# Folding the pooling heads' map into the output projection's weights on the chip, in a two-part decoder layer on one core

## The chip, the cores and the metric

One core of a Trainium2 chip runs the whole program. The metric is the device time of one execution in microseconds (us), as the median of several executions. The profiled execution is a single one; its span is the time from its first to its last instruction. The engines are named as in the profile: PE (TensorE, matrix products), DVE (VectorE, elementwise), ACT (ScalarE, activations and copies), POOL (GpSimd), SP (SyncE, which issues most transfers).

## The reference

One layer of width 1024 over 2048 positions, in float32. Cut to what the change touches:

```python
p = h @ w_in                                   # q, k, v, gate, i/f logits, and u: 512 pooling channels
hm = head_rmsnorm(mlstm_chunkwise(...), g_head) * sigmoid(o)
# multiscale_pool: 4 groups of 128 channels, windows 2, 4, 8, 16
mean = (c[:, 1:] - lag) / minimum(pos, w)      # trailing mean of the group
d = stack(mean - u_group)
y = einsum('btgc,gcd->btgd', d, w_pool)        # per-group 128 x 128 map
hp = y * pool_scale                            # per channel
x = x + concatenate([hm, hp], -1) @ w_out      # rows 512 to 1023 of w_out meet hp
```

After it come a gated feed-forward part (width 2816, convolution over positions) and a final norm. Both are untouched.

## The kernel before

Positions are worked on in four blocks (`b` = 0 to 3) of 512. For each block `in_phase` (line 531) runs four input projections, `out_proj` (926) the output projection in two halves; the feed-forward part follows at about 685 us of the profile. The order is: input phase of block 0, input phase of block 1, output projection of block 0, input phase of block 2, and so on; the last two output projections follow each other.

Every float32 product is made of three matmuls. A number is split into a rounded high part (`split_h`, line 92, on ACT) and the rest (`split_l`, 98, on DVE), and `products` (108) adds high x high, high x low and low x high in PSUM. Its three lines 112, 113 and 114 are therefore those of nearly all matmuls.

`project` (239) is the main stream: 16 steps of six matmuls (two products). Weights come in units of 128 x 2 x 512 values (512 KB). In every half of eight steps the first steps split the two units of the next half and start the loads of the two after those (`w_load`, 223, on SP, two buffers).

All other work is in generators, the side streams (`Sides`, 57). After each step `tick` advances each of them to its next `yield`, in the order in which they were added. So the order on each engine is fixed when the program is written out: a side stream's instruction stands between the projection's steps on each engine's queue. Buffers that side streams share are counted in rings (`take`, `give`, line 288): `tmp` has six buffers, `mm` two PSUM banks, `num` two, `prs` two. `take_now` spins ticks without projection steps until its slots are free.

What stands around the change:

- `setup` (451) loads small constants, waits some ticks, takes a `tmp` buffer, loads `w_pool` and splits it into `wp`.
- `norm_scale` (313) loads x and squares it, through `tmp` buffers; `qk_out` (532) evacuates the first projection, with two `tmp` buffers each; `conv` (511) gives them back after a POOL product.
- `chain` (593) computes the gates: small matmuls, DVE and ACT steps, each some ticks behind the one before, then a round trip of two rows through DRAM (`rows`), then four chunks.
- `pool_sums` (829) makes the trailing sums on POOL, subtracts the token (847) and splits the result `d` into a `prs` buffer. `pooling` (857) multiplies `wp` with it, three matmuls for each block and group, and splits the product, scaled by `pool_scale`, into the tile from which the output projection reads (`mix_tile`, 211).
- `heads_out` (879) does the like for the other half, through transposes.
- The tiles `mixT0` to `mixT7` hold that projection's input. Before they are first written, their memory holds the first weights and the first slices of x (`first_tiles`, 205).

Of the kernel before, what the change touches and what calls it, by code (L numbers as in the profile page):

```python
# [6 lines left out]
F32 = mybir.dt.float32  # L7
# [6 lines left out]
P = 128  # L14
SEQ = 2048
D = 1024
KT = D // P
# [66 lines left out]
def trunk(tc, x, xT, w_in, w_gate, w_pool, w_out, w_up, w_down, vecs, cst, out):  # L84
# [19 lines left out]
    def split(h, l, src, scale=None):  # L104
        split_h(h, src, scale)
        split_l(h, l, src, scale)

    def products(o, terms, first=True, last=True, on=False):

        n = len(terms)  # L110
        for i, ((lh, ll), (rh, rl)) in enumerate(terms):
            pe.matmul(o, lhsT=lh, rhs=rh, start=first and i == 0, stop=False, skip_group_check=on)  # L112
            pe.matmul(o, lhsT=lh, rhs=rl, start=False, stop=False, skip_group_check=on)  # L113
            pe.matmul(o, lhsT=ll, rhs=rh, start=False, stop=last and i == n - 1, skip_group_check=on)  # L114
# [7 lines left out]
    def parts(t, *idx):  # L122
        return t[(slice(None), 0) + idx], t[(slice(None), 1) + idx]
# [4 lines left out]
    with ExitStack() as ctx:  # L128
# [12 lines left out]
        def nbank(shape):  # L141
            return psum.tile(shape, F32, tag="num", name="num", bufs=2)
# [4 lines left out]
        def wait(n):  # L147
            for _ in range(n):
                yield
# [62 lines left out]
            return (hT if b == NB - 1 else mixT)[k]  # L212


        units = []
        for b in range(NB):
            units += [w_in[g, kp] for g in range(4) for kp in range(KT // 2)]
            if b:
                units += [w_out[h, kp] for h in range(2) for kp in range(KT // 2)]
        units += [w_out[h, kp] for h in range(2) for kp in range(KT // 2)]  # L220
        raws, whl = {}, {}

        def w_load(n):
# [41 lines left out]
        def until(*flag):  # L265
            while flag not in flags:
                yield
# [20 lines left out]
        def take(ring, n=1):  # L288
            while (slots := reserve(ring, n)) is None:
                yield  # L290
            return slots
# [159 lines left out]
        def setup():  # L451
            slot = reserve("tmp", 1)
            cr = tmp()
            n = C_N - C_TRI
            wgr = cr[:, n:n + KT * 8].rearrange("p (k c) -> p k c", k=KT)
            sp.dma_start(cr[:, 0:n], cst[:, C_TRI:C_N])
            sp.dma_start(wgr, w_gate)
            pool.memset(f(wg), 0.0)
            pool.memset(qk_halo, 0.0)
            for g in range(4):  # L460
                pool.memset(u[g][:, BT:], 0.0)
            pool.memset(C, 0.0)
            pool.memset(f(qd), 0.0)
            for c in chl:
                pool.memset(f(c), 0.0)
            pool.memset(m_now[:, TT:TT + 1], 0.0)
            for t in range(TT):
                pool.memset(f(va[t][:, :, :, DV:]), 0.0)
            yield from wait(8)
            split(wg[:, :, 0:8], wg[:, :, 8:16], wgr)  # L470
            for t in range(TT):
                dve.tensor_copy(va[t][:, 0, :, DV:DV + 1], ones.to_broadcast([P, H, 1]))
            dve.tensor_copy(tri, cr[:, 0:P])
            dve.tensor_copy(tab, cr[:, C_TAB - C_TRI:C_N - C_TRI].rearrange("p (g c) -> p g c", g=4))
            give(slot)
            yield from wait(16)
            slot = yield from take("tmp")
            wpr = tmp()[:, 0:512]
            sp.dma_start(wpr, w_pool)
            yield from wait(6)  # L480
            split(wp[:, 0], wp[:, 1], wpr)
            give(slot)
            yield

        def in_op(b, channels):
            def op(w, kp, j, i):
# [342 lines left out]
        def pool_sums(b):  # L829

            yield from until("u", b)
            yield from until("hs", b)
            for g, win in enumerate(WINDOWS):
                s, m, lo = u[g], 1, HALO - win + 1
                while m < win:
                    lo += m
                    slot = yield from take("tmp")
                    n = tmp()
                    pool.tensor_tensor(out=n[:, lo:], in0=s[:, lo:], in1=s[:, lo - m:HALO + BT - m], op=ALU.add)
                    if m > 1:  # L840
                        give(s_slot)
                    s, s_slot, m = n, slot, 2 * m
                    yield
                d_slot = yield from take("prs")
                if b == 0:
                    dve.tensor_tensor(out=s[:, HALO:2 * HALO], in0=s[:, HALO:2 * HALO], in1=tab[:, g], op=ALU.mult)
                dve.scalar_tensor_tensor(out=s[:, HALO:], in0=s[:, HALO:], scalar=1.0 / win, in1=u[g][:, HALO:], op0=ALU.mult, op1=ALU.subtract)
                d = ph1.tile([P, 2, BT], F32R, tag="prs", name="prs", bufs=2)
                split_h(d[:, 0], s[:, HALO:])
                yield  # L850
                split_l(d[:, 0], d[:, 1], s[:, HALO:])
                give(s_slot)
                state["d", b, g] = d, d_slot
                yield from wait(3)
                flags.add(("d", b, g))

        def pooling(b):
            if b < NB - 1:
                yield from until("op", b - 1)
            for g in range(4):  # L860
                yield from until("d", b, g)
                if b < NB - 1:
                    yield
                slot = yield from take("num")
                d, d_slot = state.pop(("d", b, g))
                o = nbank([P, BT])
                gs = slice(g * P, (g + 1) * P)
                products(o, [((wp[:, 0, gs], wp[:, 1, gs]), parts(d))])
                give(d_slot)
                yield  # L870
                m = mix_tile(b, 4 + g)
                split_h(m[:, 0], o, vec[:, V_PSC + g:V_PSC + g + 1])
                yield from wait(2)
                split_l(m[:, 0], m[:, 1], o, vec[:, V_PSC + g:V_PSC + g + 1])
                give(slot, 1)
                flags.add(("mix", b, 4 + g))
            flags.add(("pool", b))

# [102 lines left out]
        steps = setup()  # L981
        next(steps)
        sides.add(steps)
        scales = {0: sides.add(norm_scale(0))}
        for b in range(NB):
            in_phase(b)
            if b == 0:
                mixT += [per.tile([P, 2, BT], F32R, tag=f"mixT{k}", name=f"mixT{k}") for k in range(KT)]
            sides.add(pool_sums(b))
            sides.add(pooling(b))  # L990
            if b == 0:
                sides.add(heads_out(b))
            elif b < NB - 1:
                out_proj(b - 1)
                sides.add(heads_out(b))
            else:
                sides.add(heads_out(b))
                out_proj(b - 1)
# [666 lines left out]
```

## Time and profile before

| what | value |
|---|---|
| median of 3 runs | 2033.52 us (2030.06 to 2034.94) |
| profiled execution, time | 2033.21 us |
| profiled execution, span | 2031.5 us |
| DVE busy | 1455.8 us (72%) |
| ACT busy | 1023.6 us (50%) |
| POOL busy | 176.2 us (9%) |

A row of a timeline gives the start, the length, the engine, the line, the operation, the tile written and the tiles read, how often it was done in a row, and in square brackets how long the engine was idle ahead of it and who released it. Lengths of matmuls overlap; the distance between two starts is what one costs. The page gives the clock that TensorE was granted in tenths, over slices of 50.8 us:

```profile
PEclk9999999999999999999999999999999999999999
```

### The profile page before, as it was taken

Reading aid. Unit: us, or ns where it says so; the run is one execution under the profiler, and the core shown is the slowest. Engines: PE = TensorE matmul, PEld = TensorE weight load, DVE = VectorE, ACT = ScalarE, POOL = GpSimd, SP = SyncE. Lnnn points to the kernel's source line nnn. Section 1 sums busy time; section 2 is a strip of 40 time slices with the busy share of each in tenths; the row PEclk is TensorE's granted clock in tenths of the full one; section 3 lists DMA queues with packets and bytes.
Section 4 is the critical chain, followed back from the end, with each engine's and each line's share of the span. In section 5 each row is a group of like instructions: output and inputs, shape, how many; then the busy total and the mean of one; then the engine's idle time right before and its main releaser. Section 6 shows DMA issues by size and latency. Waiting matters only on the chain.

```text
span 2031.5 us, 24605 instructions
## 1 busy us (share of the span) xinstructions
PE 1976.3 (97%) x8948; PEld 1622.1 (80%) x8948; DVE 1455.8 (72%) x2371; ACT 1023.6 (50%) x1808; POOL 176.2 (9%) x224
## 2 busy tenths in 40 slices
PE   8989999998999899999999999999999999999997
PEld 6777887776787688888888888888888888888886
DVE  5587788687686978778778566588878778865443
ACT  5655655654654545545546454344544544544331
POOL 1003012111020000000000000000111111000000
PEclk9999999999999999999999999999999999999999
DMA  4433454442435522222224854432322222375341
GB/s 181 155 112 114 138 164 166 154 158 94 169 127 185 199 84 83 94 86 70 94 86 143 283 198 146 165 104 99 109 94 70 86 94 69 134 274 175 119 139 55
DMA packets 121850, 267.56 MB, mean 132 GB/s; under 512 B 10112, under 2 KB 28032, under 8 KB 121728
## 3 DMA queue, kind: packets, MB, share of 16 engines
q1 hardware_dynamic: 114528, 252.87, 37.8%
q10 hardware_dynamic: 7200, 13.11, 1.7%
q8 instruction: 70, 1.15, 0.2%
q14 instruction: 52, 0.43, 0.1%
HBM read 221.32 MB, written 44.63 MB: 131 GB/s over the span
## 4 chain that ended last, share of the span: by engine, by line
PE 80%; DVE 9%; ACT 4%; DMA 3%; issue 2%; SPq 1%; POOL 0%; DVEq 0%; ACTq 0%; POOLq 0%
PE big L112 21%; PE big L113 21%; PE big L114 21%; PE num L114 5%; PE num L113 5%; PE num L112 5%; DVE whl L100 1%; DVE tmp L519 1%; ACT hjunk L819 1%; PE mm L503 1%; DVE hT L102 1%; ACT whl L94 1%; DMA tmp<-in_x 1%; DVE so L825 0%; DVE C L785 0%
## 5 line engine op out<-in xcount | busy, mean ns | idle before, releaser
L112 PE MATMUL big<-s,w 128*128 128x512 f32 (+1 forms) x1562 | 606.1, 388 | 7.1 <-ACT r L1382 7.0
L114 PE MATMUL big<-s,w 128*128 128x512 f32 (+1 forms) x1562 | 603.9, 387 | 0.0
L113 PE MATMUL big<-s,w 128*128 128x512 f32 (+1 forms) x1562 | 603.8, 387 | 0.0
L94 ACT CAST w<-raw 128x512 fp32r<-128x512 f32 (+1 forms) x442 | 272.6, 619 | 505.0 <-PE big L114 355.5
L100 DVE TENSOR_TENSOR w<-raw,w 128x512 fp32r<-128x512 f32 (+1 forms) x442 | 302.1, 685 | 202.5 <-ACT w L94 197.4
L112 PEld LDWEIGHTS big<-s,w 128*128 128x128 f32 x1562 | 293.8, 188 | 71.3 <-ACT r L1382 9.0
L114 PEld LDWEIGHTS big<-s,w 128*128 128x128 f32 x1562 | 293.8, 188 | 60.0
L113 PEld LDWEIGHTS big<-s,w 128*128 128x128 f32 x1562 | 293.7, 188 | 58.3 <-issue 0.7
L1354 DVE SCALAR_TENSOR_TENSOR q<-q,vec 128x1024 f32<-128x1024 f32 x176 | 225.4, 1282 | 22.7 <-ACT q L1351 21.3
L112 PE MATMUL num<-s,w 128*128 128x512 f32 x396 | 154.5, 390 | 0.0
L114 PE MATMUL num<-s,w 128*128 128x512 f32 x396 | 154.2, 389 | 0.0
L113 PE MATMUL num<-s,w 128*128 128x512 f32 x396 | 154.0, 389 | 0.0
L112 PE MATMUL big<-hT,whl 128*128 128x512 f32 x320 | 128.7, 402 | 9.0 <-ACT whl L94 5.6
L100 DVE TENSOR_TENSOR whl<-wraw,whl 128x1024 fp32r<-128x1024 f32 x92 | 114.9, 1249 | 27.4 <-ACT whl L94 26.2
L100 DVE TENSOR_TENSOR s<-x,s 128x512 fp32r<-128x512 f32 x120 | 81.5, 688 | 67.7 <-ACT s L94 67.1
L94 ACT CAST s<-x 128x512 fp32r<-128x512 f32 x120 | 73.1, 619 | 109.7 <-PE big L114 41.9
L113 PE MATMUL big<-hT,whl 128*128 128x512 f32 x320 | 126.8, 396 | 0.9 <-DVE hT L102 0.9
L114 PE MATMUL big<-hT,whl 128*128 128x512 f32 x320 | 126.3, 395 | 0.0
L1375 POOL COPY q<-halo 128x2 f32<-128x2 f32 x88 | 65.3, 759 | 592.0 <-DVE q L1354 298.5
L1351 ACT ACTIVATE q<-q,vec 128x1024 f32<-128x1024 f32 x88 | 109.5, 1244 | 0.0
L112 PE MATMUL big<-whl,hT 128*128 128x512 f32 x256 | 105.6, 412 | 0.0
L113 PE MATMUL big<-whl,hT 128*128 128x512 f32 x256 | 102.7, 401 | 2.0 <-DVE whl L100 2.0
(266 smaller groups left out, 2925.3 us busy)
## 6 DMA issues: line engine op xcount, KB each, us to landing
raw<-in_w_up SPq DMA_DIRECT2D x44, 1024.0 KB, 5.6
raw<-in_w_down SPq DMA_DIRECT2D x35, 1024.0 KB, 5.1
wraw<-in_w_in SPq DMA_DIRECT2D x60, 512.0 KB, 3.4
act<-q SPq DMA_DIRECT2D x44, 512.0 KB, 6.4
x<-act SPq DMA_DIRECT2D x88, 256.0 KB, 3.8
wraw<-in_w_out SPq DMA_DIRECT2D x32, 512.0 KB, 3.5
xr<-in_xT SPq DMA_DIRECT2D x32, 256.0 KB, 4.2
x2d<-xr ACTq DMA_DIRECT2D x32, 256.0 KB, 2.9
```

What stands on the lines that cost most here:

```text
L94: act.copy(out=h, in_=src)
L100: dve.tensor_tensor(out=l, in0=src, in1=f(h), op=ALU.subtract)
L102: dve.scalar_tensor_tensor(out=l, in0=src, scalar=scale, in1=f(h), op0=ALU.mult, op1=ALU.subtract)
L112: pe.matmul(o, lhsT=lh, rhs=rh, start=first and i == 0, stop=False, skip_group_check=on)
L113: pe.matmul(o, lhsT=lh, rhs=rl, start=False, stop=False, skip_group_check=on)
L114: pe.matmul(o, lhsT=ll, rhs=rh, start=False, stop=last and i == n - 1, skip_group_check=on)
L503: pe.matmul(gp, lhsT=wg[:, k], rhs=hT[k][:, i], start=k == 0 and i == 0, stop=k == KT - 1 and i == 1)
L519: dve.scalar_tensor_tensor(out=y, in0=pre[:, n:n + BT], scalar=tap[n], in1=y, op0=ALU.mult, op1=ALU.add)
L819: act.activation(junk, nums[h // 2][:, h % 2, 0:DV], AF.Square, scale=rd[:, h:h + 1], accum_out=ssq[:, h:h + 1])
L1351: act.activation(y[gv], pre[gv][:, 2:2 + HT], AF.Identity, scale=tap[2], bias=vec[:, V_FB + ch:V_FB + ch + 1])
L1354: dve.scalar_tensor_tensor(out=y[gv], in0=pre[gv][:, n:n + HT], scalar=tap[n], in1=y[gv], op0=ALU.mult, op1=ALU.add)
L1375: pool.tensor_copy(t[:, 0:2], halo[:, gv * NJ + j])
```

## The change

Since pooling values go through two linear maps with a scale between them, `w_pool`, `pool_scale` and rows 512 to 1023 of `w_out` can be multiplied once. The new stream `fuse` does this on the chip: four units (two column halves times two pairs of groups), each loaded into a tile of `mixT`'s memory, split, multiplied with the transposed and scaled `wp` (two products for each unit), copied from PSUM by ACT and stored in DRAM (`wpo_d`). The output projection then loads these instead of the last two units of each half of `w_out`. `setup` takes its `w_pool` earlier (4 ticks in place of 16), transposes it by TensorE and splits it with the scale. `pooling` is gone; `pool_sums` splits `d` directly into the projection's input tile, without a `prs` buffer, and waits for the output projection of the block before ahead of the first split. Block 0 ends with `need("fused")`.

```diff
+        wpo_d = [[dram.tile([P, 2, 512], F32, name=f"wpo{h}_{i}") for i in range(2)] for h in range(2)]
+        out_units = [w_out[h, kp] if kp < 2 else wpo_d[h][kp - 2] for h in range(2) for kp in range(KT // 2)]
...
-            yield from wait(16)
+            yield from wait(4)
             slot = yield from take("tmp")
             wpr = tmp()[:, 0:512]
             sp.dma_start(wpr, w_pool)
             yield from wait(6)
-            split(wp[:, 0], wp[:, 1], wpr)
+
+            mm_slot = yield from take("mm")
+            wt = bank([P, BT])
+            for g in range(4):
+                pe.transpose(out=wt[:, g * P:(g + 1) * P], in_=wpr[:, g * P:(g + 1) * P], identity=ident)
             give(slot)
             yield
+            for g in range(4):
+                gs, scale = slice(g * P, (g + 1) * P), vec[:, V_PSC + g:V_PSC + g + 1]
+                split_h(wp[:, 0, gs], wt[:, gs], scale)
+            yield
+            for g in range(4):
+                gs, scale = slice(g * P, (g + 1) * P), vec[:, V_PSC + g:V_PSC + g + 1]
+                split_l(wp[:, 0, gs], wp[:, 1, gs], wt[:, gs], scale)
+            give(mm_slot)
+            flags.add(("wp",))
+            yield
+
+        def fuse():
+
+            def load(n):
+                raw = per.tile([P, 2, 512], F32, tag=f"mixT{4 * (n % 2)}", name="wor")
+                sp.dma_start(raw, w_out[n // 2, 2 + n % 2])
+                return raw
+            yield from wait(14)
+            raws2 = [load(0), load(1)]
+            yield from until("wp")
+            for n in range(4):
+                raw = raws2.pop(0)
+                res = per.tile([P, 2, 512], F32, tag=f"mixT{3 + 4 * (n % 2)}", name="wo")
+                for j in range(2):
+                    w = per.tile([P, 2, 512], F32R, tag=f"mixT{1 + 4 * (n % 2) + j}", name="wos")
+                    gs = slice((2 * (n % 2) + j) * P, (2 * (n % 2) + j + 1) * P)
+                    split_h(w[:, 0], raw[:, j])
+                    yield
+                    split_l(w[:, 0], w[:, 1], raw[:, j])
+                    yield
+                    slot = yield from take("mm")
+                    o = bank([P, 512])
+                    products(o, [(parts(wp, gs), parts(w))])
+                    yield
+                    act.copy(out=res[:, j], in_=o)
+                    give(slot)
+                del raw, w
+                act.dma_start(wpo_d[n // 2][n % 2], res)
+                del res
+                if n < 2:
+                    raws2.append(load(n + 2))
+            flags.add(("fused",))
...
                 dve.scalar_tensor_tensor(out=s[:, HALO:], in0=s[:, HALO:], scalar=1.0 / win, in1=u[g][:, HALO:], op0=ALU.mult, op1=ALU.subtract)
-                d = ph1.tile([P, 2, BT], F32R, tag="prs", name="prs", bufs=2)
+                if b < NB - 1:
+                    yield from until("op", b - 1)
+                d = mix_tile(b, 4 + g)
                 split_h(d[:, 0], s[:, HALO:])
                 yield
                 split_l(d[:, 0], d[:, 1], s[:, HALO:])
                 give(s_slot)
...
-        def pooling(b):
-            if b < NB - 1:
-                yield from until("op", b - 1)
-            for g in range(4):
-                yield from until("d", b, g)
-                if b < NB - 1:
-                    yield
-                slot = yield from take("num")
-                d, d_slot = state.pop(("d", b, g))
-                o = nbank([P, BT])
-                gs = slice(g * P, (g + 1) * P)
-                products(o, [((wp[:, 0, gs], wp[:, 1, gs]), parts(d))])
-                give(d_slot)
-                yield
-                m = mix_tile(b, 4 + g)
-                split_h(m[:, 0], o, vec[:, V_PSC + g:V_PSC + g + 1])
-                yield from wait(2)
-                split_l(m[:, 0], m[:, 1], o, vec[:, V_PSC + g:V_PSC + g + 1])
-                give(slot, 1)
                 flags.add(("mix", b, 4 + g))
             flags.add(("pool", b))
...
+        sides.add(fuse())
...
+                need("fused")
```

## Rows read from the trace of the kernel before

**Rows 1.** The page's totals: busy time, share of the span, instructions.

```profile
PE 1976.3 (97%) x8948; PEld 1622.1 (80%) x8948; DVE 1455.8 (72%) x2371; ACT 1023.6 (50%) x1808; POOL 176.2 (9%) x224
```

**Rows 2.** Timeline of PE around the first pooling product of block 0.

```profile
189.93 0.39 PE L112 MATMUL num<-prs,wp 128*128 128x512 f32 x1
...
190.62 0.60 PE L887 MATMUL mm<-ident,so 128*128 128x128 f32 x4
190.97 0.47 PE L112 MATMUL big<-whl,hT 128*128 128x512 f32 x1
```

**Rows 3.** The tile `wp`, matmuls: lengths in ns, first and last start.

```profile
L112 PE MATMUL num<-prs,wp x16: 392/393/495, 189.9 to 651.8; 128*128 128x512 f32 x16
```

**Rows 4.** Timeline of PE: pooling matmuls with idle time ahead of them.

```profile
374.54 0.49 PE L112 MATMUL num<-prs,wp 128*128 128x512 f32 x1 [1.44 <-ACT prs L94]
376.17 0.50 PE L113 MATMUL num<-prs,wp 128*128 128x512 f32 x1 [1.13 <-DVE prs L100]
...
640.43 0.49 PE L112 MATMUL num<-prs,wp 128*128 128x512 f32 x1 [1.00 <-ACT prs L94]
```

**Rows 5.** Busy time by stretch: PE, PEld, DVE, ACT, POOL, then granted clock, DMA share, GB/s.

```profile
372.00:377.10 5.10, 2.53 (x10) 1.56 (x9) 5.07 (x10) 5.10 (x11) 2.11 (x1) 1.00 0.25 75
377.20:380.50 3.30, 3.30 (x9) 2.58 (x8) 3.13 (x12) 1.21 (x6) 0.00 (x0) 0.50 0.74 230
...
506.90:513.60 6.70, 5.82 (x14) 4.57 (x15) 5.50 (x9) 3.08 (x4) 1.64 (x1) 0.50 0.36 106
```

**Rows 6.** Timeline of PE in blocks 0 and 1.

```profile
38.03 0.39 PE L112 MATMUL big<-whl,hT 128*128 128x512 f32 x1
...
47.03 0.49 PE L626 MATMUL mm<-lfs,tri 128*128 128x16 f32 x2 [2.04 <-ACT lfs L94]
...
54.13 0.27 PE L636 MATMUL mm<-ident,w 128*16 128x128 f32 x1 [1.07 <-DVE w L630]
...
62.39 0.20 PE L658 MATMUL mm<-ones,mrow 1*16 1x1 f32 x2 [0.48 <-DVE mrow L652]
...
76.73 0.38 PE L742 MATMUL mm<-ident,qk 128*128 128x128 f32 x2
...
80.72 0.50 PE L113 MATMUL big<-whl,hT 128*128 128x512 f32 x1 [1.99 <-DVE whl L100]
...
146.92 3.85 PE L503 MATMUL mm<-hT,wg 128*16 128x512 f32 x16
```

**Rows 7.** Timelines of ACT and DVE at the end of the first projection.

```profile
42.33 0.63 ACT L523 ACTIVATE tmp<-tmp 128x512 f32<-128x512 f32 x1
...
44.36 0.17 DVE L541 COPY tmp<-qk_halo 128x3 f32<-128x3 f32 x1 [1.86 <-POOL qk L528]
```

**Rows 8.** The page's groups: DVE's subtraction of a 128 x 512 split.

```profile
L100 DVE TENSOR_TENSOR w<-raw,w 128x512 fp32r<-128x512 f32 (+1 forms) x442 | 302.1, 685 | 202.5 <-ACT w L94 197.4
```

**Rows 9.** Timeline of DVE in the second projection of block 0.

```profile
54.44 0.41 DVE L641 TENSOR_TENSOR_SCAN ml<-mm,ones 16x128 f32<-16x128 f32 x1 [0.45 <-PE mm L636]
...
58.27 0.74 DVE L102 SCALAR_TENSOR_TENSOR va<-big,nr,va 128x512 fp32r<-128x512 f32 x1
...
60.62 1.20 DVE L650 COPY mrow<-mrow 1x4 f32<-1x4 f32 x1
61.74 0.60 DVE L652 TENSOR_TENSOR_SCAN mrow<-mm,mrow,br 1x4 f32<-1x4 f32 x4
```

**Rows 10.** Timelines of SP, ACT and DVE in the third projection of block 0.

```profile
73.31 0.59 SPq L319 DMA_DIRECT2D tmp<-in_x  x1
...
77.15 0.63 ACT L323 ACTIVATE tmp<-tmp 128x512 f32<-128x512 f32 x1 [5.63 <-DMA tmp<-in_x]
...
80.59 0.42 DVE L100 TENSOR_TENSOR qss<-qs,qss 128x256 fp32r<-128x256 f32 x1
```

**Rows 11.** Busy time of 40 to 66 us, columns as in rows 5; the page's transfers.

```profile
40.00:66.00 26.00, 22.41 (x100) 17.20 (x99) 19.16 (x35) 14.57 (x25) 6.08 (x4) 1.00 0.36 117
...
wraw<-in_w_in SPq DMA_DIRECT2D x60, 512.0 KB, 3.4
```

More of the change, by code (lines that the diff above doesn't have):

```diff
@@ L218, in trunk @@
             if b:
-                units += [w_out[h, kp] for h in range(2) for kp in range(KT // 2)]
-        units += [w_out[h, kp] for h in range(2) for kp in range(KT // 2)]
+                units += out_units
+        units += out_units
         raws, whl = {}, {}
@@ L843, in pool_sums @@
                     yield
-                d_slot = yield from take("prs")
                 if b == 0:
@@ L852, in pool_sums @@
                 give(s_slot)
-                state["d", b, g] = d, d_slot
-                yield from wait(3)
-                flags.add(("d", b, g))
-        def pooling(b):
-            if b < NB - 1:
-                yield from until("op", b - 1)
-            for g in range(4):
-                yield from until("d", b, g)
-                if b < NB - 1:
-                    yield
-                slot = yield from take("num")
-                d, d_slot = state.pop(("d", b, g))
-                o = nbank([P, BT])
-                gs = slice(g * P, (g + 1) * P)
-                products(o, [((wp[:, 0, gs], wp[:, 1, gs]), parts(d))])
-                give(d_slot)
-                yield
-                m = mix_tile(b, 4 + g)
-                split_h(m[:, 0], o, vec[:, V_PSC + g:V_PSC + g + 1])
-                yield from wait(2)
-                split_l(m[:, 0], m[:, 1], o, vec[:, V_PSC + g:V_PSC + g + 1])
-                give(slot, 1)
                 flags.add(("mix", b, 4 + g))
@@ L987, in trunk @@
             if b == 0:
+                need("fused")
                 mixT += [per.tile([P, 2, BT], F32R, tag=f"mixT{k}", name=f"mixT{k}") for k in range(KT)]
             sides.add(pool_sums(b))
-            sides.add(pooling(b))
             if b == 0:
```

## The prediction

> **What bounds the kernel now.** I read the page's totals first, then TensorE's timeline with its idle time, then the rows of the pooling matmuls, then the DVE, ACT and SP timelines of the first 90 us. TensorE is busy for 97% of the span [rows 1], so a matmul less is worth its own pitch as long as nothing else is late at that place. The duration of a matmul in the rows is not its pitch, since matmuls overlap: three pooling matmuls start at 189.93 and the next group starts at 190.62, so a product of three costs 0.69 us [rows 2]. The rest of the span is 55 us of idle time, and it lies in a few places, of which two kinds matter here: the pooling matmuls themselves [rows 4], and the first block, where the small matmuls of the gate chain wait for DVE and ACT [rows 6]. The reader should also see the granted clock: after idle stretches of TensorE it falls to 0.50, which is 1.2 GHz, for 3.3 us and for 6.7 us [rows 5]. A stall can so cost twice.
>
> **What the change removes.** The pooling map ran 16 times, three matmuls each [rows 3]: 16 x 0.69 = 11.0 us of TensorE. With them go the waits of these matmuls for their operand, 1.44, 1.13 and 1.00 us [rows 4], together 3.6 us, and the stretch at half clock right behind the first two [rows 5], 3.3 us in which half the work was done, so 1.6 us. These 5.2 us are uncertain. In 372 to 377.1 DVE and ACT are busy nearly without a break [rows 5], so TensorE may meet the same backlog one matmul later; the ends are 0 and 5.2, and I take 5.2, because the split that the pooling matmul waited for leaves TensorE's path altogether. ACT and DVE each lose 16 splits of 128 x 512. I count those as nothing, since neither engine is the bound over these blocks; in the DVE pile-up around 505 to 514 us [rows 5] the pooling splits go, but the last group's sums come earlier, into the same pile; I count 0, with 5 us either way in the range. The new wait in `pool_sums` for the previous output projection holds one `tmp` slot for a few steps; behind it wait only later pool groups, and their result is needed an input projection later, so 0. At the end of the first stage (block 3) the pooled halves are ready earlier; that gives the 1.00 us already counted.
>
> **What the change adds on TensorE.** Four units of two products each: 8 x 0.69 = 5.5 us; four transposes 0.35 us, as the four of 190.62 to 190.97 [rows 2]. Together 5.9 us. The work alone thus gives 11.0 - 5.9 = 5.1 us back.
>
> **Where the added products stand.** This is the step on which the prediction hangs. The side streams are emitted one step per tick, and a tick follows six projection matmuls, twice 0.69, so 1.38 us. `setup` waits 8 + 4 ticks, takes a `tmp` slot (free), loads `w_pool`, waits 6 and so reaches the transposes at tick 18. The third `qk_out` needs that same slot and spins three ticks until then; before, the fourth one spun three ticks for a conv slot. Both versions therefore leave the first projection at tick 20, and the gate chain keeps its places. The flag `wp` comes at tick 20, and `fuse` splits at ticks 20 and 21 and multiplies at 22, then every third tick: 25, 28, 31, 34, 37, 40, 43. A product stands one tick, 1.38 us, behind the DVE subtraction that it needs, and DVE works in order.
>
> First product, tick 22. TensorE gets there two steps into the second projection: 38.03 + 0.35 + 2 x 1.38 = 41.1 us [rows 6]. DVE is then held by the fourth `qk_out`, which needs a buffer that the first conv slice frees on POOL: it resumes at 44.36, behind ACT's sigmoid and its table load [rows 7]. That dependency stays, perhaps 0.7 us earlier. Behind it come the `qk_out` product, four small subtractions for `wp` and the subtraction of the unit (0.69 each) [rows 8]: some 2.6 us, so 46.3. TensorE waits 46.3 - 41.1 = about 5 us. Ends: 3.5 and 6.
>
> At ticks 25 and 28 the operands are there in time, since TensorE has now fallen back. The chain's own waits of 2.04, 1.07 and 0.48 us [rows 6] vanish for the same reason.
>
> Fourth product, tick 31. The chain's scan waits for a matmul of tick 29, then DVE has in order the scan, three conv operations, a weight subtraction and the `va` subtraction, 54.44 to 58.9 [rows 9], and now the unit's 0.69 behind them: 5.2 us from the matmul. TensorE has two steps, 2.8 us, until it needs it: a stall of about 2.5.
>
> Fifth product, tick 34. DVE has a `va` subtraction behind the projection's evacuation, the two operations of 1.20 and 0.60 us of the running maximum [rows 9], a weight subtraction of 1.2 and the unit's own: a stall of about 2.
>
> Eighth product, tick 43. Before, ACT sat idle for 5.63 us until 77.15 for a load of x [rows 10], which SP issued at 73.31 [rows 10] because it was held behind the gate rows' round trip through DRAM. DVE got through with what was queued behind that at about 81.0 [rows 10], while TensorE passed the place of tick 43 one step ahead of the transposes of 76.73 [rows 6], at 75.3. The loads of x run one tick pair earlier without `setup`'s late slot, but the one that ACT needs at tick 40 still follows the rows. With ACT's copy and split and DVE's subtraction behind it I get 81.7 against 75.3; TensorE will come later by about 10 us and the rows by about 9, so a stall of about 5. Ends 2 and 6.5. The 1.99 us at 80.72 [rows 6] go with it.
>
> Sum of the stalls: 5 + 2.5 + 2 + 5 = 14.5, less the 2.04 + 1.07 + 0.48 + 1.99 = 5.6 that they replace: 8.9 us. Ends: 0, if DVE and ACT are ahead of TensorE by these 14.5 us in a way that I don't see, and 13.
>
> The clock: 2.57 us of idle time in 372 to 377.1 was followed by 3.3 us at half clock, and the stall ahead of 507 by 6.7 us [rows 5], while the 2.04 us at 47.03 had no such stretch behind them. Two stalls of 5 us should each be followed by one, at 1.7 to 3.4 us. I take 4 us for both, ends 0 and 8.
>
> **The four loads and stores of the fused units** move 4 MB over some 60 us, on SP's and ACT's queues. In 40 to 66 us the DMA engines are busy for 0.36 [rows 11], so I count 0; SP meets no new long wait, because the tiles that it loads into are free by then. The Trainium skill ("Trainium Kernel Development and Optimization", Key Constraints) says that transfers issued from SP's and ACT's queues all run on the same 16 DMA engines and interleave, which speaks against a count of nothing: each weight unit behind a fused load would land later. By that rule one weight unit late by a landing of another, 3.4 us in the profile's list of issues [rows 11], would cost that much and make the result 2039. The share of 0.36 shows room, so the sum goes by 0.
>
> **Sum against the profiled execution**, which took 2033.2 us with a span of 2031.5; the median of the runs is 0.3 us above: -11.0 - 5.2 + 5.9 + 8.9 + 4 = +2.6. I predict 2036 us.
>
> **Rivals.** (A) The cover holds: DVE and ACT deliver the units in time and only the count of matmuls moves. For it: DVE and ACT are idle between many of their rows, and the first block has buffers to run ahead. Against it: the chain's waits at 47, 54 and 62 us [rows 6], with four or more ticks of distance where the products have one. Time: 2033.2 - 11.0 + 5.9 - 5.2 = 2023, or 2028 if the waits of the pooling matmuls come back elsewhere. (B) Slower: the ladder of stalls in the first block at its upper ends, each stall of 5 us followed by the longer stretch at half clock. 2033.2 - 11.0 + 5.9 + 13 + 8 = 2049 with nothing won at the pooling matmuls, 2044 with it; in the middle 2043. It decides once the first block loses over 22 us, against 19 in my sum. For it: in-order queues make each delay wait for TensorE's next step, and the first block has no slack that gives it back. (C) The stalls come as forecast, but the DVE pile-up at 505 us, with its stretch of 6.7 us at half clock, thins out because the last pool group's POOL additions no longer run under it: 5 us better, 2031.
>
> **How the numbers follow.** Forecast 0.40, with 2030 to 2039 as its own range; A 0.20; B 0.28; C 0.12. This kernel's measurement tells about 0.3%, 6.1 us, from no change: faster below 2027.4, slower above 2039.6. A lies mostly below (0.16 of its 0.20), B above; the forecast leaks 0.02 to each side. Faster 0.18, same 0.52, slower 0.30. The range of 2023 to 2045 leaves out half of A and a quarter of B.
>
> **What would show it.** In the changed kernel: 48 matmuls with `wp` as weights gone from blocks 0 to 3 and 24 there between 41 and 95 us; idle rows of TensorE ahead of products with result tile `mm`, released by DVE or ACT, of about 5, 2.5, 2 and 5 us; a granted clock of 0.50 behind the first and the last; the 16 gate matmuls of block 1, at 146.92 before [rows 6], later by 15 to 22 us, and the rest of the first stage then shorter by some 16. If the fused products show no idle time ahead of them, the step with the ticks is wrong and A holds.

## The result, and the profile after

The changed kernel takes 2042.63 us (median of 6 runs, 2037.49 to 2044.54), the kernel before beside it 2031.8 us (6 runs). The ratio is 1.0054, with a 95% interval of [1.0042, 1.0065]: slower by some 11 us, by more than the 0.3% that the prediction set as its bound. The predicted 2036 us is 6.6 us too low; the time lies inside the stated 2023 to 2045 and outside the forecast's own 2030 to 2039. The profiled execution took 2043.11 us, with a span of 2041.4 against 2031.5, so 9.9 us longer.

The page's totals after, to be read against [rows 1]:

```profile
PE 1976.8 (97%) x8928; PEld 1621.1 (79%) x8928; DVE 1453.4 (71%) x2366; ACT 1023.1 (50%) x1811; POOL 175.1 (9%) x224
```

There are twenty matmuls fewer, as the diff says (48 less 28), and yet TensorE is busy for as long as before: the work saved was eaten by work done slowly. To see where, I cut the first stage at the first matmul of each projection on TensorE's timeline. Lengths are in us. In the kernel before, the four pooling products of a block, three matmuls each, ran while the next block was worked on. The first column of numbers is the change that the prediction's terms give. Below, "block 0" stands for the first of these stretches, "block 1" for the second.

| stretch | predicted | before | after | change |
|---|---|---|---|---|
| block 0, second and third projection | +18.8 | 53.6 | 67.5 | +13.8 |
| block 0, fourth projection, and block 1 | -2.8 | 151.1 | 146.5 | -4.7 |
| output projection of block 0 | 0 | 59.4 | 59.2 | -0.3 |
| block 2 | -7.0 | 106.7 | 118.8 | +12.1 |
| output projection of block 1 | 0 | 60.7 | 58.5 | -2.2 |
| block 3 | -2.8 | 114.8 | 108.6 | -6.2 |
| last two output projections | -3.8 | 102.1 | 102.4 | +0.3 |

Before these stretches 0.9 us were won, and in the feed-forward part 2.2.

**Block 0.** Timeline of PE, the fused products with idle time ahead of them:

```profile
44.41 0.80 PE L112 MATMUL mm<-wos,wp 128*128 128x512 f32 x1 [4.38 <-ACT wos L94]
...
64.89 0.50 PE L113 MATMUL mm<-wos,wp 128*128 128x512 f32 x1 [1.92 <-DVE wos L100]
...
71.19 0.50 PE L113 MATMUL mm<-wos,wp 128*128 128x512 f32 x1 [0.92 <-DVE wos L100]
...
77.16 0.50 PE L113 MATMUL mm<-wos,wp 128*128 128x512 f32 x1 [0.57 <-DVE wos L100]
...
88.62 0.50 PE L112 MATMUL mm<-wos,wp 128*128 128x512 f32 x1 [1.44 <-ACT wos L94]
89.52 0.50 PE L113 MATMUL mm<-wos,wp 128*128 128x512 f32 x1 [0.40 <-DVE wos L100]
```

The waits of [rows 6] at 47, 54, 62 and 81 us are gone, and in their place stands the forecast ladder. Busy time by stretch (columns as in [rows 5]) shows the clock behind its first and its last stall, and, in the last three lines, in block 2:

```profile
43.60:50.40 6.80, 5.99 (x13) 4.43 (x14) 5.36 (x10) 4.40 (x8) 1.88 (x1) 0.50 0.33 102
88.60:95.40 6.80, 6.38 (x28) 5.02 (x29) 2.76 (x5) 3.90 (x9) 0.32 (x1) 1.00 0.48 162
...
333.70:337.10 3.40, 3.40 (x9) 2.67 (x9) 3.30 (x6) 1.70 (x3) 2.12 (x2) 0.50 0.49 141
354.20:357.60 3.40, 3.15 (x9) 2.52 (x10) 2.54 (x6) 1.89 (x3) 0.68 (x1) 0.50 0.72 228
384.90:391.70 6.80, 5.90 (x16) 4.63 (x16) 6.11 (x17) 4.25 (x10) 0.00 (x0) 0.50 0.56 189
```

Behind the stall of 4.38 us TensorE ran at 0.50, that is 1.2 GHz, for 6.8 us; behind the last stall, 1.44 and 0.40 us at 89, it stayed at 2.4 GHz.

**Block 2** is the surprise. Timeline of PE there; before, the block's waits were 0.45, 0.35 and the two of [rows 4], 3.4 us together, with one stretch of 3.3 us at half clock:

```profile
333.40 0.36 PE L674 MATMUL mm<-lfs,tri 128*128 128x16 f32 x2 [1.65 <-DVE mixT L102]
...
354.45 0.21 PE L686 MATMUL mm<-bs,ident 128*1 128x16 f32 x2 [4.29 <-DVE mixT L102]
...
384.57 0.54 PE L112 MATMUL big<-whl,hT 128*128 128x512 f32 x1 [3.73 <-ACT whl L94]
386.01 0.79 PE L113 MATMUL big<-whl,hT 128*128 128x512 f32 x1 [0.90 <-DVE whl L100]
```

All idle time of the block is 11.2 us, so 7.9 more; the stretches at half clock are 13.6 us, 10.2 more, at half the work 5.1 us lost. Less the twelve pooling matmuls (2.8) that makes 10.2 of the 12.1. The rest is work of the side streams: twenty matmuls of a chunk that stood in the output projection of block 1 before, which is 2.2 us shorter for it.

Two differences show in the trace. The first is the order on POOL and DVE. In the kernel before, the pool groups had to take the two `prs` buffers. One addition of the third group ran under the fourth convolution, the two others at 350.47, and the fourth group began at 353.30, behind the last POOL product of the convolutions:

```profile
340.48 3.91 DVE L519 SCALAR_TENSOR_TENSOR tmp<-tmp,vec 128x512 f32<-128x512 f32 x3
```

```profile
342.46 1.38 POOL L839 TENSOR_TENSOR tmp<-u 128x518 f32<-128x518 f32 x1
348.69 1.83 POOL L528 TENSOR_TENSOR qk<-tmp 128x512 f32<-128x512 f32 x1 [4.85 <-ACT tmp L523]
...
353.30 1.06 POOL L839 TENSOR_TENSOR tmp<-u 128x526 f32<-128x526 f32 x1 [0.33 <-ACT tmp L323]
```

In the changed kernel the fourth group begins as soon as the third is through, at 303.01 us, and its other three additions run at 336.58, 343.26 and 349.60, among the convolutions at the turn from the first to the second projection. Timelines of DVE (three convolution steps in a row, a triple) and of POOL (the product after a convolution, L576, and the additions, L887):

```profile
327.66 2.33 DVE L567 SCALAR_TENSOR_TENSOR tmp<-tmp,vec 128x512 f32<-128x512 f32 x3 [0.85 <-ACT tmp L591]
...
334.60 3.92 DVE L567 SCALAR_TENSOR_TENSOR tmp<-tmp,vec 128x512 f32<-128x512 f32 x3
...
340.50 3.23 DVE L567 SCALAR_TENSOR_TENSOR tmp<-tmp,vec 128x512 f32<-128x512 f32 x3
...
348.26 4.26 DVE L567 SCALAR_TENSOR_TENSOR tmp<-tmp,vec 128x512 f32<-128x512 f32 x3
```

```profile
303.01 1.93 POOL L887 TENSOR_TENSOR tmp<-u 128x526 f32<-128x526 f32 x1
334.90 1.59 POOL L576 TENSOR_TENSOR qk<-tmp 128x512 f32<-128x512 f32 x1 [29.97 <-ACT tmp L571]
336.58 1.39 POOL L887 TENSOR_TENSOR tmp<-tmp 128x524 f32<-128x524 f32 x1
...
349.60 1.59 POOL L887 TENSOR_TENSOR tmp<-tmp 128x512 f32<-128x512 f32 x1
```

The four triples take 13.7 us; where POOL does nothing one takes 2.33. In the kernel before the same four took 2.33, 2.31, 2.69 and 3.91, so 11.2. The second difference is a load of x. ACT waited for one there before, too, and waits longer now. ACT's timeline before and after, and that of SP's queue after:

```profile
369.67 0.63 ACT L323 ACTIVATE tmp<-tmp 128x512 f32<-128x512 f32 x1 [6.67 <-DMA tmp<-in_x]
```

```profile
380.22 0.63 ACT L325 ACTIVATE tmp<-tmp 128x512 f32<-128x512 f32 x1 [8.94 <-DMA tmp<-in_x]
```

```profile
370.71 0.34 SPq L748 DMA_DIRECT2D mb<-rows  x1
...
373.06 1.23 SPq L750 DMA_DIRECT2D eb<-rows  x2
374.34 0.59 SPq L321 DMA_DIRECT2D tmp<-in_x  x1
```

SP issues the load of x at 374.34, only after the gate rows' round trip through DRAM; ACT waits 8.94 us for it, with the casts of the weight units and of the chunk behind it, and TensorE waits for a weight unit at 384.57.

**Block 3** gave 6.2 us back. Timeline of PE before, with 6.7 us at half clock among these waits [rows 5], and at the same place after:

```profile
505.11 0.20 PE L638 MATMUL mm<-bs,ident 128*1 128x16 f32 x2 [3.08 <-DVE mixT L102]
...
507.78 1.22 PE L163 MATMUL mm<-sh,ones_r 128*128 128x512 f32 x2 [2.47 <-DVE ml L641]
...
516.45 0.17 PE L647 MATMUL mm<-ident,ml 16*1 16x16 f32 x1 [1.11 <-DVE ss L171]
```

```profile
522.91 0.20 PE L686 MATMUL mm<-bs,ident 128*1 128x16 f32 x2 [0.58 <-DVE mixT L102]
524.36 0.84 PE L163 MATMUL mm<-sh,ones_r 128*128 128x512 f32 x2 [1.25 <-DVE ml L689]
...
531.89 0.17 PE L695 MATMUL mm<-ident,ml 16*1 16x16 f32 x1 [1.11 <-DVE ss L171]
```

**The last two output projections** were forecast 3.8 us shorter and are not. The wait of 1.00 us [rows 4] is gone, but waits of 1.46 and 1.39 us for the other half of the projection's input came in at 651 and 654, with 3.4 us at half clock.

### The profile page after: what moved, and what is told of

The parts are those of the page before. It is cut to its first block, busy times and chain, and to the rows that moved or that the text cites. A ratio compares the mean times of both kernels' runs of the same rounds, so it can differ in the third digit from the quotient of the medians.

```text
span 2041.4 us, 24585 instructions
## 1 busy us (share of the span) xinstructions
PE 1976.8 (97%) x8928; PEld 1621.1 (79%) x8928; DVE 1453.4 (71%) x2366; ACT 1023.1 (50%) x1811; POOL 175.1 (9%) x224
## 4 chain that ended last, share of the span: by engine, by line
PE 74%; DVE 12%; ACT 6%; DMA 4%; issue 3%; SPq 1%; ACTq 0%; POOL 0%; DVEq 0%
PE big L112 20%; PE big L113 19%; PE big L114 19%; PE num L114 5%; PE num L113 5%; PE num L112 5%; DVE whl L100 2%; DVE tmp L567 1%; DMA xr<-in_xT 1%; ACT whl L94 1%; ACT hjunk L867 1%; DMA x2d<-xr 1%; DVE hT L102 1%; DVE so L873 1%; PE mm L551 1%
## 5 line engine op out<-in xcount | busy, mean ns | idle before, releaser
L113 PEld LDWEIGHTS big<-s,w 128*128 128x128 f32 x1562 | 293.9, 188 | 58.5 <-issue 0.7
L1402 POOL COPY q<-halo 128x2 f32<-128x2 f32 x88 | 64.9, 754 | 593.0 <-DVE q L1381 298.3
```

The source lines that it names most:

```text
L1402: pool.tensor_copy(t[:, 0:2], halo[:, gv * NJ + j])
```

## The experiments

Each kernel's ratio to the kernel before, which was measured again beside it, stands with its interval; two tables of stretches follow the last one. The ratios rest on several executions, each stretch and each row on a single profiled one.

**The pool side alone.** `setup` as before, no `fuse`, the output projection loads `w_out` as it is: the map and its scale are left out of the computation.

```diff
-        out_units = [w_out[h, kp] if kp < 2 else wpo_d[h][kp - 2] for h in range(2) for kp in range(KT // 2)]
+        out_units = [w_out[h, kp] for h in range(2) for kp in range(KT // 2)]
...
-        sides.add(fuse())
...
-                need("fused")
```

> Leaves out the multiplication of the weights: no stream fuse, no transposed map (setup as in the kernel before), and the output projection loads its rows of w_out as they are, so the pooling map is missing from the output. It is the pooling side of the change alone. Theory (ladder): the first block is as before to within 1 us, and the pooling side alone brings only some 3 us, 2029, because block 2 loses about 10 us in its first two input projections, whatever happened in block 0. Rival (knock-on): block 2's loss comes only from the lateness that block 0 passes on; then the pooling side brings 13 to 16 us, 2016 to 2019.

Measured: 2029.38 us, ratio 0.9987 [0.9979, 0.9996], as the theory said. Sixteen products fewer and nothing added in the first block brings 2.6 us, not 11 to 16; by the ratios the fuse then costs the other 13.6. The stalls of block 2 are there without any fused product, so the fuse is not their cause:

```profile
343.78 0.20 PE L672 MATMUL mm<-bs,ident 128*1 128x16 f32 x2 [4.30 <-DVE mixT L102]
...
372.77 0.51 PE L112 MATMUL big<-whl,hT 128*128 128x512 f32 x1 [2.49 <-ACT whl L94]
```

**The fuse without its products.** The eight products are left out, and ACT copies the raw rows instead; loads, splits, copies and stores stay, so the map is left out of the computation.

```diff
-                    o = bank([P, 512])
-                    products(o, [(parts(wp, gs), parts(w))])
...
-                    act.copy(out=res[:, j], in_=o)
+                    act.copy(out=res[:, j], in_=raw[:, j])
```

> As the changed kernel, but the eight products of fuse are left out; ACT copies the loaded rows instead of the product, so that the splits, the copies, the loads and the stores all stay. The pooling map is missing from the output. Theory (ladder): TensorE's order is the cause, not the load on ACT, DVE or the transfers; without the products block 0 loses 2 us or less against the kernel before, in place of 14, and the time is about 2031. Rival (load): the added ACT and DVE work and 4 MB of transfers delay the gate chain and the weight splits; block 0 still loses 8 us or more, and the time stays above 2037.

Measured: 2032.3 us, ratio 1.0005 [0.9995, 1.0015]. The same work on DVE, ACT and the queues costs block 0 2.8 us in place of 13.8, a little more than the theory's 2 and far from the rival's 8. So the load on the other engines is the small part of the price. Of the 11 us that go, some 5.5 are the work of the eight products (0.69 us each), the rest is what their place in TensorE's order costs.

**The products one period later.** Each unit's product is issued three ticks further on, behind the splits of the next one (`finish` holds the product, the copy, the store and the next load); nothing is left out.

```diff
...
+                    if ready:
+                        yield from finish(*ready)
+                    else:
+                        yield
+                    ready = n, j, w, res
...
```

> The same work as the changed kernel; each product of fuse is written out one period later, so it stands four ticks behind its DVE subtraction instead of one. Theory (ladder): the idle time ahead of these products falls from 9.6 us to under 2, the stretch of 6.8 us at half clock behind the first one goes, some of the gate chain's old waits of 2.0 and 1.1 us come back, and block 0 loses 6 to 8 us instead of 14: about 2035. Rival (load): no change beyond 2 us, 2041 to 2043.

Measured: 2037.37 us, ratio 1.003 [1.0018, 1.0042]. The ladder shrinks to one stall, the one that hangs on the load of x in block 0 (ACT waits 6.98 us for it), and block 0 to 62.9 us. That is 9.3 more than before and not the 6 to 8 expected, since the stretch of 6.8 us at half clock did not go; it now stands behind this stall:

```profile
83.41 0.80 PE L112 MATMUL mm<-wos,wp 128*128 128x512 f32 x1 [4.09 <-ACT wos L94]
```

**The fourth pool group held back** in blocks 1 and 2, until `qk_out` of the next block is through:

```diff
+                if g == 3 and 0 < b < NB - 1:
+                    yield from until("qk", b + 1)
```

> As the changed kernel, but in blocks 1 and 2 the fourth pooling group starts only when the short convolution of the next block is done, about where it ran before the change. Theory (POOL under the convolution): DVE's three convolution operations go back from 3.2 to 4.3 us to some 2.3 to 3.3, the idle time of 4.3 us near 354 us and the one of 3.7 us near 384 us shrink to what the kernel before had (0.5 and 2.6), and one or two stretches at half clock go with them: about 2034. Rival (order of the pooling splits on DVE and ACT, or the late load of x, not POOL): block 2 keeps its loss, 2041 to 2043.

Measured: 2037.34 us, ratio 1.0028 [1.0019, 1.0037]. The four convolution triples of block 2 take 2.33, 3.24, 2.32 and 3.38 us, 11.3 together as in the kernel before, and the stall of 4.29 us is gone: the early place of this group was its cause. The edit moves the group's POOL additions, its `tmp` buffers and its part on DVE and ACT together, so which of them made the stall isn't shown apart. The block is not shorter for it (118.5 us): other matmuls wait now.

```profile
363.88 0.20 PE L706 MATMUL mm<-ones,mrow 1*16 1x1 f32 x2 [1.82 <-DVE mrow L700]
...
387.21 1.40 PE L373 MATMUL mm<-prs,ones_r 128*128 128x512 f32 x2 [4.49 <-DVE prs L368]
...
407.98 0.36 PE L112 MATMUL num<-chl,qss 128*128 128x260 f32 x1 [2.58 <-DVE C L833]
```

Ahead of the second of them ACT waits 9.45 us for a load of x. The gain of the whole run, some 5 us by the ratios, is not in this block; in the profile the output projection of block 1 is 3.2 us shorter and the feed-forward part 2.4, block 3 is 2.7 longer.

**Loads of x on ACT's queue** for all blocks but the first, so that they don't stand behind the gate rows' round trip on SP:

```diff
-                sp.dma_start(xt, x[(b * TT + n // 2) * P:(b * TT + n // 2 + 1) * P, n % 2 * 512:(n % 2 + 1) * 512])
+                (act if b else sp).dma_start(xt, x[(b * TT + n // 2) * P:(b * TT + n // 2 + 1) * P, n % 2 * 512:(n % 2 + 1) * 512])
```

> As the changed kernel, but the loads of x for the norm scales of blocks 1 to 3 are issued by ACT, so they are no longer queued on SP behind the round trip of the gate rows. Theory: ACT's waits of 5.6 to 8.9 us for such a load end, and with them the idle time of TensorE ahead of the eighth product (1.8 us) and near 384 us (3.7 and 0.9 us) and the half-clock stretch behind the latter: 2042.6 - 6.4 - 3.4, about 2033; at least 2037. Rival: the load is late because the DMA engines are busy, not because of SP's queue; no change, 2041 to 2043.

Measured: 2032.97 us, ratio 1.0002 [0.9992, 1.0011], as the theory said. One line brings the kernel back to the time of the kernel before. The sixth load of the block, the one that SP issued at 374.34, leaves beside the rows' round trip and not behind it; its square no longer waits, and the first chunk's cast waits for the gate rows alone. ACT's timeline and queue:

```profile
363.88 0.36 ACTq L321 DMA_DIRECT2D tmp<-in_x  x1
...
367.54 0.64 ACT L325 ACTIVATE tmp<-tmp 128x512 f32<-128x512 f32 x1
...
372.27 0.41 ACT L94 CAST ks<-qk 128x256 fp32r<-128x256 f32 x1 [4.00 <-DMA eb<-rows]
```

The stall of 3.73 us at 384.57 is gone. Block 2 is 7 us shorter, although the stall under the convolution is still there, even longer:

```profile
351.37 0.21 PE L686 MATMUL mm<-bs,ident 128*1 128x16 f32 x2 [5.41 <-DVE mixT L102]
```

**The same line in the kernel before**, as a control:

> The kernel before with the same move of the loads of x to ACT and nothing else: a control for what that move is worth without the change. Theory: its waits near 80.7 us (2.0) and 374 to 376 us (2.6, with 1.6 at half clock) go: about 2026. Rival: the move changes nothing, 2031.

Measured: 2021.94 us, ratio 0.9948 [0.9933, 0.9963], more than expected. ACT's waits for x of 5.63 [rows 10] and 1.42 us in block 0 and of 6.67 in block 2 shrink to 1.19, 0 and 0:

```profile
75.52 0.63 ACT L323 ACTIVATE tmp<-tmp 128x512 f32<-128x512 f32 x1 [1.19 <-DMA tmp<-in_x]
```

So the load was late in the kernel before too, and moving it is worth the same 0.52% in both kernels. Measured against this control, the fold with the same line (2032.97) loses 11 us still: the late load explains none of the difference between the two kernels as a whole. Only its place differs. In block 2 the line is worth 6.9 us in the changed kernel and 1.5 in the kernel before, where most of its 10 us lie outside blocks 0 and 2, for reasons that I haven't traced.

**Products later and x on ACT's queue:**

> The changed kernel with each product of fuse one period later and the loads of x on ACT. Theory: the remaining idle time of 4.1 us ahead of the last product in the spread kernel, with 6.8 us at half clock behind it, and block 2's stall near 380 us go: 2037.4 - 4.1 - 3.4 - 3.4, about 2027 to 2030. Rival: these stalls return at another operand, 2035 or more.

Measured: 2027.75 us, ratio 0.998 [0.9971, 0.9989]. The two gains add up: by the ratios they are 0.24% and 0.52% apart and 0.74% together.

**All three edits:**

> The changed kernel with spread products, loads of x on ACT and the fourth pooling group of blocks 1 and 2 behind the next block's convolution. Theory: if the three repairs are independent, 2042.6 - 5.3 - 5.3 (as each measured alone) - 5 (loads of x) = 2027; if the late fourth group only pushes its work into the next pile, the same as spread_x.

Measured: 2023.47 us, ratio 0.9948 [0.9932, 0.9965]. That is less than the 2027 of the theory, faster than both kernels, and no faster than the control. The gains add up here too: 0.24%, 0.52% and 0.26% apart, 1.06% together. In its profile these waits are left, with 13.6 us at half clock behind them:

```profile
355.93 0.21 PE L718 MATMUL mm<-ones,mrow 1*16 1x1 f32 x2 [2.80 <-DVE mrow L712]
...
392.58 0.36 PE L112 MATMUL num<-chl,qss 128*128 128x260 f32 x1 [2.61 <-DVE C L845]
...
516.87 0.18 PE L707 MATMUL mm<-ident,ml 16*1 16x16 f32 x1 [3.86 <-DVE ss L171]
```

**The fourth group eight and twenty ticks later still:**

```diff
                     yield from until("qk", b + 1)
+                    yield from wait(8)
```

> The kernel with all three edits, and the fourth pool group of blocks 1 and 2 held for eight ticks more (about 11 us), so that its POOL additions run behind the running maximum of the gate chain, near 365 us, and not at 350 to 357 us. Theory (in block 2 it matters under which DVE work these additions run): the stall of 2.80 us ahead of the running maximum's matmul at 356 us and the half clock behind it (3.4 us) go, the block takes about 108 us in place of 112.6, and the kernel takes about 2019 us. Rival (each place of the additions only exchanges one stall for another, since DVE is late by the same amount anyway): block 2 stays at 112 to 113 us, and the time at 2023.

> As the run with eight ticks, with twenty (about 28 us): the additions fall behind the chain's first chunk, near 380 us, and the operand is split shortly ahead of the output projection at 415 us. Theory: as good as eight ticks or a little worse, 2019 to 2022, with a new stall only where the split comes under the chunks' DVE work. Rival: 2023 or more, with a stall of 2 to 4 us among the chunk matmuls at 380 to 405 us.

Measured: 2023.51 us, ratio 0.9962 [0.9949, 0.9975], with eight ticks, and 2031.63 us, ratio 0.9992 [0.9981, 1.0004], with twenty. With eight ticks the stall of 2.80 us falls to 0.67, but waits of 1.06 and 1.44 us come in at 370 and 375 us and the 2.61 stays: block 2 is 1.7 us shorter, and the run as a whole is not. My theory of 2019 failed; the rival's time was right, its block length nearly. With twenty ticks, where the rival was right too, the last additions run at 393 us, the waits among the chunks are 1.42 and 2.61 us, and block 3 has five waits of 0.9 to 1.85 us between 557 and 586 us and is 3.4 us longer than in the kernel with all three edits. So at the three places tried, the place of the group decided which matmul waits, more than whether one does.

The stretches of the earlier table, from one profile of each kernel; the columns are in the order of the runs:

| stretch | before | after | pool side alone | no products | later products | group 4 held | x on ACT |
|---|---|---|---|---|---|---|---|
| block 0 | 53.6 | 67.5 | 53.4 | 56.4 | 62.9 | 66.7 | 64.9 |
| block 1 | 151.1 | 146.5 | 149.8 | 147.9 | 146.5 | 146.7 | 145.3 |
| block 2 | 106.7 | 118.8 | 116.9 | 116.1 | 116.8 | 118.5 | 111.9 |
| output projection of block 1 | 60.7 | 58.5 | 60.2 | 60.2 | 58.6 | 55.4 | 58.5 |
| block 3 | 114.8 | 108.6 | 108.6 | 108.6 | 108.6 | 111.3 | 108.6 |

| stretch | before, x on ACT | later products, x on ACT | all three | 8 ticks | 20 ticks |
|---|---|---|---|---|---|
| block 0 | 51.7 | 58.6 | 57.2 | 56.8 | 57.5 |
| block 1 | 149.5 | 146.8 | 147.7 | 145.1 | 147.7 |
| block 2 | 105.2 | 111.2 | 112.6 | 110.9 | 113.5 |
| output projection of block 1 | 59.9 | 60.1 | 55.4 | 55.4 | 55.8 |
| block 3 | 114.7 | 108.6 | 111.4 | 111.3 | 114.8 |

The feed-forward part, whose program is the same in all of them, takes 1340.4 to 1345.0 us in these profiles, so a microsecond or two in one stretch of one profile decides nothing.

## Why the prediction was right or wrong

The time lies in the stated range, but partly by luck: two errors offset each other, block 0 better than forecast and the later blocks much worse. By the pool side alone, the change's two sides are worth -2.6 and +13.6 us. The prediction had -16.2 for what the change removes and +18.8 for what it adds.

**Block 0: right in kind, a third too high.** There are 24 matmuls with `wp` between 44.4 and 89.9 us. The stalls came at the four forecast places, released by ACT or DVE; 5, 2.5, 2 and 5 us were predicted, and 4.4, 1.9, 0.9 and 1.8 came, with 0.6 at a place not named. All idle time of the stretch is 9.6 us against 5.6 before, so the term of +8.9 measured +4.0. The most mis-sized part is the last product: ACT's wait for x ahead of it was 2.96 us, not 5.63 as in [rows 10]. The clock term of 4 measured 3.4 (6.8 us at half clock behind the first stall, none behind the last). What is left of the 13.8 us, 6.4, is the work of 26 more matmuls in the stretch, against 5.9 forecast. The gate matmuls of block 1 came 10.9 us later, not 15 to 22.

**Counting the loads of the fused units as nothing: right.** No cast of a weight unit waits for its load between 30 and 110 us, and the landing of the input weights takes 3.5 us against 3.4 [rows 11]. The Trainium skill ("Trainium Kernel Development and Optimization", Key Constraints) says that transfers of all queues share the same 16 DMA engines and interleave; in these rows that costs next to nothing. The 2039 us drawn from it come nearer the result than 2036, but not through that mechanism.

**The step that failed: the pool work moved for nothing.** The prediction said of the wait in `pool_sums` that "behind it wait only later pool groups", so 0, and took 5.2 us of waits as won. That looked at when the result is needed and not at what ran at the time to which POOL's and DVE's part moves. The two `prs` buffers had been a brake: in the kernel before, the fourth group's additions started at 353.3 us, behind all four convolutions (their POOL products end at 350.5). In the changed kernel they stand between the convolutions. Block 2, forecast at -7.0, measured +12.1. The pool side alone shows the same, +10.2, so this loss comes from the pool work and not from the fuse. Why it is so dear is shown only in part. The late load of x makes some 5.4 us of it, the difference between what its move is worth in block 2 of the two kernels. The early fourth group makes the stall of 4.29 us; but holding it back doesn't shorten the block, because other matmuls wait in its place, and with all three edits the block is still 7.4 us longer than in the control. I had seen the load of x as a cost in block 0 [rows 10] and not asked where else the same queue was late.

**Rival C was half right.** The pile-up at 505 us thinned out by the mechanism named there: the last additions moved from 500.66 us, under the convolution, to 489.75 and 494.01, ahead of it. Block 3 gained 6.2 us, 3.4 beyond the matmuls, where 5 were priced. The same move in block 2 put three of them under it; I saw the gain in one block and not the loss in the other.

**Rival B had the sign and not the reason.** It decided from 22 us lost in the first block; 13.8 were lost. What was slower than forecast was a later block, by a mechanism that no rival had. The errors then offset each other: block 0 was 5.0 us better than forecast, the stretches from block 1 to the feed-forward part together 15.6 us worse (-0.8 against -16.4), and 3.1 us were won in parts that the sum left out.

**What stays open.** With its stalls treated, the fold stands at 2023.5 us and the control at 2021.9, although its matmuls are fewer by 5.1 us' worth. The tables of stretches say where the gain goes (block 2 is 7.4 us longer than in the control, block 3 and the output projection of block 1 7.8 shorter, block 0 5.5 longer); none of the three places that I tried for the fourth group won it back, and whether another order of the side streams would isn't settled.

## What to carry to other kernels

A buffer ring that is taken away may have been what kept two engines' bursts apart: of work that is moved, write down beside which operations of each engine it will run, in every repetition of the block, not only when its result is due. Where a side stream's product is put into an in-order matmul queue, a distance of one step from the elementwise work that feeds it is too short when that engine's queue holds several microseconds; the same products three steps later cost 5 us less. And when a change loses through a wait, look whether the wait existed before: here one load moved to another engine's queue was worth 10 us in both kernels, twice what the fold could have saved. Without the same line in the kernel before, it would have passed for the cure of the change's loss.

## What the runs showed of the hardware beyond that

POOL's work and DVE's lengthen each other. A convolution triple on DVE takes 2.33 us alone. At 334.60 us it takes 3.92, so 1.59 more, with a POOL product of 1.59 us and an addition of 1.39 under it. Where no DVE instruction runs, such a product takes 1.29 us (43.04 us in the kernel before) and an addition 1.04 (292.49 us in the changed kernel), so these two lose 0.65 together. The Trainium skill ("SBUF — State Buffer", section "SBUF: two separate sides") says that VectorE and GpSimd share a pair of ports which one instruction holds whole, so that the other waits, also where a VectorE operation reads two inputs from SBUF against a GpSimd operation that reads there, as both do here. The rows agree in that both engines lose time, but show less than a full wait: one behind the other the five instructions would take 2.33 and 2.33, so 4.66 us, and they were through in 3.92.

A stall was paid twice, as forecast, but not in proportion. Up to 720 us the stretches at half clock add up to 20.5 us in the kernel before and 34.1 after, so 6.8 us of work lost of the 9.9. Their length doesn't follow that of the stall alone: 4.38 us at 44 us were followed by 6.8 us at 1.2 GHz, 4.29 us at 354 by 3.4 us, and 1.65 us at 333 by 3.4 us, where 1.84 us at 89 had none. Nor does the same wait always cost the same: in the output projection of block 1 waits of 1.18 and 1.83 us were followed by 3.4 us at half clock with the pool side alone, and nearly the same two, 1.19 and 1.83, by none in the changed kernel.

Moving the load of x to ACT's queue gave 0.52% in either kernel. The Trainium skill ("Trainium Kernel Development and Optimization", Key Constraints) says that issuing from several engines saves only the issue time. These rows show more: the issue takes 0.3 to 0.6 us, but ACT waited 5.63, 6.67 and 8.94 us for a load that stood in SP's queue behind transfers that wait, and with the move the three waits shrink to 1.19, 0 and 0.
